# An encoder trunk with 64 experts: gate and up weights as one load of 16 KB a partition instead of two of 8 KB, expert rows read back four at a time

## The chip, the cores and the metric

One core of a Trainium2 chip runs the whole program. The metric is the device time of one execution in microseconds; the time of a kernel is the median of several runs.

## The reference, cut to what matters

Two layers over 512 tokens of width 1024, all in float32. Each layer has a token mixer (attention and spatial gating, not touched here) and a mixture of experts:

```python
scores = sigmoid(xt @ router_w)              # 512 tokens, 64 experts
sel = scores + router_bias                   # best 4 of 8 groups, then best 8 experts
wts = scores[eidx] / sum * 2.5
hb = silu(xb @ w_gate[e]) * (xb @ w_up[e])   # 1024 -> 256, for the tokens of expert e
yb = (hb @ w_down[e]) * wts                  # 256 -> 1024
routed = segment_sum(yb, token)
shared = (silu(xt @ ws_gate) * (xt @ ws_up)) @ ws_down
x = layer_norm(ALPHA * x + gate2 * (routed + shared), ln2_g, ln2_b)
```

Every expert has 2 MB of gate and up weights and 1 MB of down weights, so a layer's experts are 192 MB.

## The kernel before, in words

The instruction order of every engine is the order in which the program is written (`manual_schedule`); the tile framework adds the semaphores. All weight loads are issued by SyncE, one after the other, each waiting until the buffer that it overwrites has been read for the last time.

**Units.** The experts, ranked by load, have fixed capacities (`CAPS`). `_units` packs them into 43 units of 128 token rows: a unit is one expert with 128 rows, or two experts that share the rows (64 and 64, or 96 and 32). An expert with more than 128 rows, or one whose rows are cut, lies in two neighbouring units. The order of the units is set by `_units` from the planner's figures of line 49, so that units with much to load alternate with units with little: one unit of one expert stands at the front (`FIRSTS`), three at the end (`ENDS`).

**A unit's work** is in the loop of lines 1188 to 1221, one unit ahead in its first half: step `u_` does gate/up of unit `u_` and down of unit `u_ - 1`. In order on TensorE: at even steps the transposes of a pair's gathered rows (`turn_pair`, line 1025) and the slot matmuls of a later pair (`bring_pair`, line 1041, which also starts that pair's gathers on GpSimd, line 1046); gate/up over the first four of eight slices of 128 input columns (`gate_up` with half 0, line 770); the transposes of the unit before (`turn`, line 783); gate/up over the other four slices; then the down matmuls of the unit before (`down`, line 796). ScalarE and VectorE make silu and product (lines 775, 777), VectorE scales the result (line 802), and GpSimd scatters the rows to DRAM, one row for each token and choice (`ysl`, line 1062).

**Loads.** `get(r, part)` (line 760) loads a part of an expert's weights the first time that it is asked for: parts 0 and 1 are the two halves of gate and up, each 128 partitions of 8 KB, and part 2 is down, 128 partitions of 8 KB. `gate_up` asks for part 0 ahead of its first half and for part 1 ahead of its second (line 766), `down` for part 2 (line 791). SyncE so issues, for a step, the first halves of the unit's experts, their second halves, and the down weights of the unit before. The first eight loads of a layer are issued earlier, as soon as the experts' order is known (`AHEAD`, line 938).

**Buffers** (`wnew`, line 740). Gate/up tiles take turns in six buffers of 8 KB a partition (`w` in pool `bring`) and, once the overflow loop of line 1122 is past, two more (`w2` in pool `ch`, `MORE`). Down tiles have three buffers of 8 KB (`wd`). The router's weights take one of the six (line 690), the shared expert's gate and up two.

**Read-back.** After the last scatter that counts, `collect` (line 1178) loads the eight rows of each token again, two rows of 1024 at a time: 16 loads of 128 partitions of 8 KB, in the gate/up buffers. For each of the four token tiles (line 1236) VectorE adds the rows of the first two loads (line 1246), TensorE sums the other two by identity matmuls (line 1250) with the last two units' rows (line 1242), and VectorE adds that and normalises. In layer 1 the rows of the norm's weights are loaded after the read-back (lines 1227 and 1228), and VectorE and GpSimd apply them (lines 1232 and 1233).

Of the kernel before, what the change touches and what calls it, by code (L numbers as in the profile page):

```python
# [12 lines left out]
F32 = mybir.dt.float32  # L13
# [14 lines left out]
TOP = 8  # L28
# [11 lines left out]
PRE = 1  # L40
FIRSTS = 1
ENDS = 3
MORE = 2
AHEAD = 8
assert len(CAPS) == E


# [79 lines left out]
UNITS = _units()  # L127
# [48 lines left out]
def trunk(tc, A):  # L176
    nc = tc.nc
# [13 lines left out]
    act, dve, gp, pe = nc.scalar, nc.vector, nc.gpsimd, nc.tensor  # L191
# [9 lines left out]
    ident = kc[:, C_ID:C_ID + 128]  # L201
# [142 lines left out]
    def mixer(l, st):  # L344
# [54 lines left out]
        if l == 0:  # L399
            load, add, total = st["ada"]  # L400
            ws = [t[:, k] for t in (am.tile([128, 4, 2, 512], F32, tag="oa", name="wa1"),
                                    att.tile([128, 4, 2, 512], F32, tag="T16a", name="wa0")) for k in range(4)]
# [10 lines left out]
        if l == 0:  # L413
            ps = psum()
# [97 lines left out]
        for kv in range(2):  # L512
            for part in range(2):
                ps = psum(F32R)
# [172 lines left out]
        att.release()  # L687
        bring = pool("bring", "right")
        st["bring"] = bring
        t = bring.tile([128, 2048], F32, tag="w", bufs=6, name="rw")  # L690
        rw, rb = t[:, 0:NK * E].rearrange("p (k e) -> p k e", k=NK), t[:, NK * E:(NK + 1) * E]
        gp.dma_start(rw, A["router_w"][l])
        gp.dma_start(rb, A["router_bias"][l:l + 1, :].to_broadcast([128, E]))
# [28 lines left out]
    def moe(l, st):  # L722
# [17 lines left out]
        def wnew(part):  # L740
            if part == 2:
                return bp.tile([128, 2048], F32, tag="wd", bufs=WD_BUFS, name="wd")
            if more:
                more[0] += 1
                if more[0] % (6 + MORE) >= 6:
                    return more[1].tile([128, 2048], F32, tag="w2", bufs=MORE, name="we")
            return bring.tile([128, 2048], F32, tag="w", bufs=6, name="we")

        def load(which, part):
            t = wnew(part)  # L750
            if which == "shared":
                src = A["w_sh"][l, part]
            else:
                if which not in regs:
                    regs[which] = nc.sync.value_load(eid[0:1, which:which + 1], min_val=0, max_val=E - 1)  # L755
                src = A["w_exp"][l, ds(regs[which], 1), part].rearrange("o p n -> p (o n)")
            nc.sync.dma_start(t, src)  # L757
            return t

        def get(r, part):  # L760
            if (r, part) not in weights:
                weights[r, part] = load(r, part)
            return weights[r, part]

        def gate_up(xT, segs, half, ps):
            ws = [get(r, half) for r, _, _, _ in segs]
            for kk in range(4):
                k = half * 4 + kk
                for s, c, m in _tiles(segs):
                    pe.matmul(ps[c:c + m, :], xT[:, k, c:c + m], ws[s][:, kk * 512:(kk + 1) * 512],  # L770
                              start=k == 0, stop=k == NK - 1)

        def swiglu(ps, n):
# [49 lines left out]
        def shared_down(i):  # L823
            down(sh_h[i], SH, 128, None, ysh[:, i])

        for part in range(3):
            get("shared", part)
        pss = turn_x(range(NK))
        for i in range(NT):
# [105 lines left out]
        pe.matmul(pr[0:1, 0:E], kc[0:E, C_ECOL:C_ECOL + 1], perm[0:E, 0:E], start=True, stop=True)  # L935
        pe.matmul(pr[0:E, 64:65], perm[0:E, 0:E], ck[0:E, 1:2], start=True, stop=True)
        dve.tensor_copy(eid, pr[0:1, 0:E])
        for r, part in [(s[0], part) for u in UNITS[:3] for s in u for part in range(3)][:AHEAD]:
            get(r, part)
        px = psum()  # L940
        for i in range(NT):
# [180 lines left out]
        with tc.For_i(0, nov, 1) as j:  # L1122
            rv = dve.value_load(ovr[0:1, ds(j, 1)], min_val=0, max_val=E - 1)
            rs_ = nc.sync.value_load(ovr[0:1, ds(j, 1)], min_val=0, max_val=E - 1)
            dve.tensor_copy(cur, PW[:, :, ds(rv, 1)].rearrange("p i o -> p (i o)"))
            dve.tensor_copy(off, ovo[:, ds(j, 1)])
            dve.tensor_scalar(cur, cur, off, None, op0=OP.subtract)
            es = nc.sync.value_load(eid[0:1, ds(rs_, 1)], min_val=0, max_val=E - 1)
            for part in range(3):
                t = wnew(2) if part == 2 else ch.tile([128, 2048], F32, tag="w2", bufs=MORE, name="we")  # L1130
                nc.sync.dma_start(t, A["w_exp"][l, ds(es, 1), part].rearrange("o p n -> p (o n)"))
                weights["over", part] = t
            segs = [("over", 0, 0, 128)]
            P = bp.tile([128, NT, 256], F32R, tag="P", bufs=2, name="P")
            onehot(segs, P, 0, lambda r: cur[:, :, None])
            wc, idx, _ = slots(P, 0, segs, rv, rowbuf[:, 0])
            xg = bp.tile([128, NK, 256], F32, tag="xg", bufs=2, name="xg")
            gather([rowbuf[:, 0]], xg)
            ps = psum()
            gate_up(xg[:, :, 0:128], segs, 0, ps)  # L1140
            gate_up(xg[:, :, 0:128], segs, 1, ps)
            t = turn(swiglu(ps, 128), 128)
            y = down(t, segs, 128, wc)
            scatter(y, idx)
# [33 lines left out]
        def collect():  # L1178

            for i in range(NT):  # L1180
                for a in range(TOP // 2):
                    t = wnew(0).rearrange("p (j d) -> p j d", j=2)
                    src = ysl[l].rearrange("(t j) d -> t j d", j=TOP)
                    nc.sync.dma_start(t, src[i * 128:(i + 1) * 128, 2 * a:2 * a + 2, :])
                    got.append(t)

        got = []
        for u_ in range(n_units + 1):
            if u_ % 2:
                mark_pair(u_ // 2 + 3)  # L1190
            else:
                if u_:
                    turn_pair(u_ // 2 + 1) if units_of(u_ // 2 + 1) else None
                bring_pair(u_ // 2 + 2)
            if u_ < n_units:
                ps = psum()
                xT = G[u_][0]
                gate_up(xT, UNITS[u_], 0, ps)
            if u_ >= 1:
                t = turn(H[u_ - 1], rows_of(UNITS[u_ - 1]))  # L1200
            if u_ < n_units:
                gate_up(xT, UNITS[u_], 1, ps)
                H[u_] = swiglu(ps, rows_of(UNITS[u_]))
            if u_ == 0:
                turn_pair(1)
            if u_ >= 1:
                _, wc, idx, tk = G.pop(u_ - 1)
                if u_ - 1 >= n_units - LATE:
                    PT = late_mark(tk)
                y = down(t, UNITS[u_ - 1], rows_of(UNITS[u_ - 1]), wc)  # L1210
                if u_ - 1 < n_units - LATE:
                    scatter(y, idx)
                else:
                    late(y, PT)
                if u_ == n_units - LATE:
                    for v_ in range(u_, n_units):
                        for r, _, _, _ in UNITS[v_]:
                            for part in range(3):
                                get(r, part)
                    collect()  # L1220
                drain(slow, 3)
# [12 lines left out]
            nc.sync.dma_start(A["out"][i * 128:(i + 1) * 128, :], x[:, i])  # L1234

        for i in range(NT):
            mine = got[i * TOP // 2:(i + 1) * TOP // 2]
            fin = [psum() for _ in range(2)]
            for n, (PT, yg) in enumerate(lates):
                for a in range(2):  # L1240
                    for h in range(2):
                        pe.matmul(fin[h], PT[:, i * 128:(i + 1) * 128], yg[:, a, h * 512:(h + 1) * 512],  # L1242
                                  start=n == 0 and a == 0, stop=False)
            for t in mine[:2]:
                for j in range(2):
                    dve.tensor_tensor(x[:, i], x[:, i], t[:, j], op=OP.add)  # L1246
            for n, t in enumerate(mine[2:]):
                for j in range(2):
                    for h in range(2):
                        pe.matmul(fin[h], ident, t[:, j, h * 512:(h + 1) * 512], start=False, stop=n == 1 and j == 1)  # L1250
            for h in range(2):
                hs = slice(h * 512, (h + 1) * 512)
                dve.tensor_tensor(x[:, i, hs], fin[h], x[:, i, hs], op=OP.add)
            normalise(x[:, i], [x[:, i, h * 512:(h + 1) * 512] for h in range(2)], 1e-5, True, both=i == NT - 1)
            if last and i:
                affine(i - 1)
# [80 lines left out]
def _pack(inputs):  # L1337
# [21 lines left out]
    def expert(g, u, d):  # L1359
        lead = g.shape[:-2]  # L1360
        n = len(lead)
        gu = np.concatenate([g.reshape(*lead, 2, 4, 128, 256), u.reshape(*lead, 2, 4, 128, 256)], -1)
        gu = np.moveaxis(gu, n + 2, n + 1).reshape(*lead, 2, 128, 2048)
        dd = np.moveaxis(d.reshape(*lead, 1, 2, 128, 1024), n + 2, n + 1).reshape(*lead, 1, 128, 2048)
        return np.concatenate([gu, dd], n)

    out = {
        "kc": _consts(),
# [13 lines left out]
        "lnc": np.stack([f(n).reshape(L, NK, 128) for n in ("ln1_g", "ln1_b", "ln2_g", "ln2_b")], 1)  # L1382
        .transpose(3, 0, 1, 2).reshape(128, L * 4 * NK),
        "router_bias": f("router_bias"),
        "w_exp": expert(f("w_gate"), f("w_up"), f("w_down")),
        "w_sh": expert(f("ws_gate"), f("ws_up"), f("ws_down")),
    }
    return {k: np.ascontiguousarray(v) for k, v in out.items()}

# [11 lines left out]
```

## Time and profile before

| | before |
|---|---|
| median of 3 runs | 2148.94 us (2147.86 to 2150.25) |
| profiled execution | 2151.45 us, its span 2149.7 us |
| TensorE busy (PE) | 1999.3 us, 93% |
| weight loads of TensorE busy (PEld) | 1109.6 us, 52% |
| VectorE busy (DVE) | 1001.3 us, 47% |
| ScalarE, GpSimd busy (ACT, POOL) | 495.6 and 372.8 us |
| mean granted TensorE clock | 0.978 of full speed |
| loads of expert weights | 384 of 1 MB (256 of gate/up, 128 of down) |
| read-back loads | 32 of 1 MB |
| bytes moved by DMA | 626.30 MB |

The expert stages lie at about 455 to 1040 us (layer 0) and 1497 to 2077 us (layer 1); ahead of each is a mixer and the routing. Busy times are of engines, not of the chain that sets the end. A row such as `PE ps L770 <- DMA we<-in_w_exp` reads: TensorE's instruction of line 770, which writes `ps`, waited until the load of `we` from `in_w_exp` had landed. `q1` is SyncE's DMA queue, `q0` GpSimd's (gathers and scatters), and each load is spread over 16 DMA engines.

### The profile page before, as it was taken

Reading aid. Unit: us, or ns where it says so; the run is one execution under the profiler, and the core shown is the slowest. Engines: PE = TensorE matmul, PEld = TensorE weight load, DVE = VectorE, ACT = ScalarE, POOL = GpSimd, SP = SyncE. Lnnn points to the kernel's source line nnn. Section 1 sums busy time; section 2 is a strip of 40 time slices with the busy share of each in tenths; the row PEclk is TensorE's granted clock in tenths of the full one; section 3 lists DMA queues with packets and bytes.
Section 4 is the critical chain, followed back from the end, with each engine's and each line's share of the span. In section 5 each row is a group of like instructions: output and inputs, shape, how many; then the busy total and the mean of one; then the engine's idle time right before and its main releaser. Section 6 shows DMA issues by size and latency. Waiting matters only on the chain. (4 is left out here: it accounts for less than half of the span.)

```text
span 2149.7 us, 29249 instructions
## 1 busy us (share of the span) xinstructions
PE 1999.3 (93%) x10868; PEld 1109.6 (52%) x10868; DVE 1001.3 (47%) x2155; ACT 495.6 (23%) x983; POOL 372.8 (17%) x353
## 2 busy tenths in 40 slices
PE   5999999989999999999999999998999999999993
PEld 4888888443333433233488888854433334333341
DVE  6777857443332332222678665653333223232245
ACT  3464232111111111111145633321111111111110
POOL 1101101027111111111230010111631111111113
PEclk9999999989999999999999999998999999999997
DMA  7513665458999999999953045525899999999983
GB/s 276 186 40 119 211 210 197 160 209 359 408 404 407 422 392 406 417 410 376 391 177 118 16 154 164 192 78 210 349 405 408 409 410 421 392 411 401 419 363 155
DMA packets 120128, 626.30 MB, mean 291 GB/s; under 512 B 19472, under 2 KB 19472, under 8 KB 65968
## 3 DMA queue, kind: packets, MB, share of 16 engines
q1 hardware_dynamic: 92912, 550.99, 65.2%
q0 software_dynamic: 27072, 73.42, 9.2%
q8 instruction: 87, 1.43, 0.3%
q14 instruction: 57, 0.47, 0.1%
HBM read 596.02 MB, written 51.38 MB: 301 GB/s over the span
## 5 line engine op out<-in xcount | busy, mean ns | idle before, releaser
L770 PE MATMUL ps<-we,xg 128*32 128x512 f32 (+2 forms) x3648 | 670.0, 602 | 28.9 <-DMA we<-in_w_exp 28.7
L770 PEld LDWEIGHTS ps<-we,xg 128*32 128x32 f32 (+2 forms) x3648 | 210.1, 124 | 385.0 <-issue 295.4
L796 PE MATMUL ps<-wd,hTt 128*32 128x512 f32 (+2 forms) x1888 | 374.5, 603 | 25.9 <-DMA wd<-in_w_exp 22.6
L777 DVE TENSOR_TENSOR h<-h,ps 128x256 f32<-128x256 f32 x94 | 39.6, 421 | 597.7 <-ACT h L775 597.7
L796 PEld LDWEIGHTS ps<-wd,hTt 128*32 128x32 f32 (+2 forms) x1888 | 118.7, 127 | 259.0 <-issue 200.0
L1062 POOL DMA_INDIRECT ysl<-y,ii x82 | 88.1, 1075 | 788.0 <-DVE y L802 717.4
L802 DVE SCALAR_TENSOR_TENSOR y<-ps,wc,r 128x512 f32<-128x512 f32 x172 | 129.2, 751 | 201.3 <-PE ps L796 201.3
L299 PE MATMUL ps<-wH,hH 128*128 128x512 f32 (+1 forms) x512 | 197.1, 385 | 4.1 <-ACT hH L194 4.1
L300 PE MATMUL ps<-wL,hH 128*128 128x512 f32 (+1 forms) x512 | 194.8, 380 | 0.0
L301 PE MATMUL ps<-wH,hL 128*128 128x512 f32 (+1 forms) x512 | 194.5, 380 | 0.0
L194 ACT ACTIVATE hTt<-ps 128x256 f32<-128x256 f32 x94 | 36.1, 384 | 497.5 <-PE ps L783 497.5
L194 ACT ACTIVATE wH<-w 128x1024 fp32r<-128x1024 f32 x83 | 87.8, 1060 | 204.0 <-PE ps L301 129.7
L1032 ACT ACTIVATE xg<-ps,f 128x256 f32<-128x256 f32 (+1 forms) x176 | 84.2, 557 | 213.3 <-DVE xg L1034 213.3
L1046 POOL DMA_INDIRECT rowbuf<-xd,it x86 | 87.9, 1022 | 227.7 <-DVE it L1045 187.9
L296 DVE TENSOR_TENSOR wL<-w,wH 128x1024 fp32r<-128x1024 f32 x84 | 102.5, 1221 | 51.7 <-ACT wH L194 51.7
L775 ACT ACTIVATE h<-ps 128x256 f32<-128x256 f32 x94 | 36.1, 384 | 346.4 <-PE ps L770 346.4
L237 DVE SCALAR_TENSOR_TENSOR acc<-wa,cond,acc 128x1024 f32<-128x1024 f32 x80 | 106.7, 1333 | 9.5 <-DMA wa<-in_w_ada 4.8
L299 PEld LDWEIGHTS ps<-wH,hH 128*128 128x128 f32 x512 | 97.8, 191 | 23.9 <-ACT hH L194 5.2
L301 PEld LDWEIGHTS ps<-wH,hL 128*128 128x128 f32 x512 | 97.6, 191 | 18.8 <-DVE hL L296 0.9
L300 PEld LDWEIGHTS ps<-wL,hH 128*128 128x128 f32 x512 | 98.0, 191 | 17.9 <-issue 0.5
L1025 PEld LDWEIGHTS ps<-kc,rowbuf 128*128 128x128 f32 x688 | 75.9, 141 | 34.5 <-PE ps L796 17.4
L1025 PE MATMUL ps<-kc,rowbuf 128*128 128x128 f32 x688 | 84.1, 275 | 3.6 <-DMA rowbuf<-xd,it 3.6
(326 smaller groups left out, 2378.4 us busy)
## 6 DMA issues: line engine op xcount, KB each, us to landing
we<-in_w_exp SPq DMA_DIRECT2D x256, 1024.0 KB, 17.6
wd<-in_w_exp SPq DMA_DIRECT2D x128, 1024.0 KB, 16.6
wa<-in_w_ada SPq DMA_DIRECT2D x96, 512.0 KB, 4.5
w<-in_wA SPq DMA_DIRECT2D x92, 512.0 KB, 4.3
we<-ysl SPq DMA_DIRECT2D x32, 1024.0 KB, 12.4
we<-in_w_sh SPq DMA_DIRECT2D x4, 1024.0 KB, 9.4
xd<-x SPq DMA_DIRECT2D x8, 512.0 KB, 2.6
x<-in_x SPq DMA_DIRECT2D x4, 512.0 KB, 10.8
```

What stands on the lines that cost most here:

```text
L194: return act.activation(out, in_, AF.Copy)
L237: dve.scalar_tensor_tensor(acc, w, cond[:, k:k + 1], acc, op0=OP.mult, op1=OP.add)
L296: dve.tensor_sub(l_out, src, h_out.bitcast(F32))
L299: pe.matmul(ps, aH, wH, start=first, stop=False)
L300: pe.matmul(ps, aH, wL, start=False, stop=False)
L301: pe.matmul(ps, aL, wH, start=False, stop=last)
L770: pe.matmul(ps[c:c + m, :], xT[:, k, c:c + m], ws[s][:, kk * 512:(kk + 1) * 512], start=k == 0, stop=k == NK - 1)
L796: pe.matmul(ps[c:c + m, :], t[:, j, c:c + m], ws[s][:, j * 1024 + nh * 512:j * 1024 + (nh + 1) * 512], start=j == 0, stop=j == 1)
L802: dve.scalar_tensor_tensor(y[0:n, hs], ps[0:n], wcol[0:n], gate2[0:n, hs], op0=OP.mult, op1=OP.mult)
L1025: pe.transpose(ps[:, kk * 256 + b_ * 128:kk * 256 + (b_ + 1) * 128], r[:, (k2 * 2 + kk) * 128:(k2 * 2 + kk + 1) * 128], ident)
L1046: gp.indirect_dma_start(out=row, out_offset=None, in_=xd, in_offset=IndirectOffsetOnAxis(ap=it[:, 0:1], axis=0), bounds_check=T - 1, oob_i ...
L1062: gp.indirect_dma_start(out=ysl[l], out_offset=IndirectOffsetOnAxis(ap=ii[:, 0:1], axis=0), in_=y, in_offset=None, bounds_check=T * TOP - ...
```

## The change

Gate and up of an expert are packed as one array, so that a partition holds the eight slices of 512 columns in 16 KB, and down is an array of its own. A gate/up tile is 16 KB a partition; there are three and one of them instead of six and two. `gate_up` asks for the whole tile ahead of its first half. The first loads of a layer are five (three of 2 MB, two of 1 MB) instead of eight. The read-back loads four rows at a time, so a token tile has two loads: one for VectorE, one for TensorE.

```diff
-MORE = 2
-AHEAD = 8
+MORE = 1
+AHEAD = 5
...
-        t = bring.tile([128, 2048], F32, tag="w", bufs=6, name="rw")
+        t = bring.tile([128, 4096], F32, tag="w", bufs=3, name="rw")
...
                 more[0] += 1
-                if more[0] % (6 + MORE) >= 6:
-                    return more[1].tile([128, 2048], F32, tag="w2", bufs=MORE, name="we")
-            return bring.tile([128, 2048], F32, tag="w", bufs=6, name="we")
+                if more[0] % (3 + MORE) >= 3:
+                    return more[1].tile([128, 4096], F32, tag="w2", bufs=MORE, name="we")
+            return bring.tile([128, 4096], F32, tag="w", bufs=3, name="we")
...
             t = wnew(part)
+            of = "gu" if part == 0 else "d"
             if which == "shared":
-                src = A["w_sh"][l, part]
+                src = A["w_sh_" + of][l]
...
-                src = A["w_exp"][l, ds(regs[which], 1), part].rearrange("o p n -> p (o n)")
+                src = A["w_exp_" + of][l, ds(regs[which], 1)].rearrange("o p n -> p (o n)")
...
-            ws = [get(r, half) for r, _, _, _ in segs]
+            ws = [get(r, 0) for r, _, _, _ in segs]
...
-                    pe.matmul(ps[c:c + m, :], xT[:, k, c:c + m], ws[s][:, kk * 512:(kk + 1) * 512],
+                    pe.matmul(ps[c:c + m, :], xT[:, k, c:c + m], ws[s][:, k * 512:(k + 1) * 512],
...
-        for part in range(3):
+        for part in (0, 2):
             get("shared", part)
...
-                for a in range(TOP // 2):
-                    t = wnew(0).rearrange("p (j d) -> p j d", j=2)
+                for a in range(TOP // 4):
+                    t = wnew(0).rearrange("p (j d) -> p j d", j=4)
                     src = ysl[l].rearrange("(t j) d -> t j d", j=TOP)
-                    nc.sync.dma_start(t, src[i * 128:(i + 1) * 128, 2 * a:2 * a + 2, :])
+                    nc.sync.dma_start(t, src[i * 128:(i + 1) * 128, 4 * a:4 * a + 4, :])
...
-            mine = got[i * TOP // 2:(i + 1) * TOP // 2]
+            mine = got[2 * i:2 * i + 2]
...
-            for t in mine[:2]:
-                for j in range(2):
+            for t in mine[:1]:
+                for j in range(4):
                     dve.tensor_tensor(x[:, i], x[:, i], t[:, j], op=OP.add)
-            for n, t in enumerate(mine[2:]):
-                for j in range(2):
+            for t in mine[1:]:
+                for j in range(4):
                     for h in range(2):
-                        pe.matmul(fin[h], ident, t[:, j, h * 512:(h + 1) * 512], start=False, stop=n == 1 and j == 1)
+                        pe.matmul(fin[h], ident, t[:, j, h * 512:(h + 1) * 512], start=False, stop=j == 3)
```

The same two parts instead of three are asked for in the first loads (line 938), in the overflow loop (line 1129) and ahead of the read-back (line 1218). On the host `expert` (line 1359) returns the two arrays.

## Rows read from the trace of the kernel before

**Rows 1.** The page, part 2: busy tenths in 40 slices.

```profile
PE   5999999989999999999999999998999999999993
...
DMA  7513665458999999999953045525899999999983
```

**Rows 2.** Transfers, 530 to 1020 us: GB/s in 40 slices; queue: packets, MB, share.

```profile
GB/s 405 422 417 424 364 420 424 421 380 385 423 419 423 355 426 422 420 422 418 421 421 351 353 423 421 369 419 413 410 422 422 396 421 409 410 421 423 372 406 287
...
q1 hardware_dynamic: 23469, 170.90, 84.7%
q0 software_dynamic: 10151, 26.80, 13.8%
```

**Rows 3.** Waits of PE, 530 to 1020 us: total us, times, longest.

```profile
PE ps L770 <- DMA we<-in_w_exp: 14.2, 12, 2.4
PE ps L796 <- DMA wd<-in_w_exp: 11.2, 9, 2.2
```

**Rows 4.** Waits of SyncE's queue, 530 to 1020 us: total us, times, longest.

```profile
SPq L757 <- PE ps L796: 205.9, 29, 13.2
```

**Rows 5.** SyncE's issues, 560 to 600 us: start, us from first to last.

```profile
568.45 0.86 SPq L757 DMA_DIRECT2D we<-in_w_exp  x2
569.55 15.25 SPq L757 DMA_DIRECT2D wd<-in_w_exp  x2
```

**Rows 6.** Timeline of PE, 560 to 600 us: start, us, what, [idle before].

```profile
570.71 5.34 PE L770 MATMUL ps<-we,xg 128*64 128x512 f32 x14 [2.42 <-DMA we<-in_w_exp]
575.98 0.44 PE L783 MATMUL ps<-kc,h 128*128 128x128 f32 x2
576.35 3.97 PE L770 MATMUL ps<-we,xg 128*64 128x512 f32 x16
...
581.63 3.65 PE L796 MATMUL ps<-wd,hTt 128*64 128x512 f32 x14 [0.78 <-DMA wd<-in_w_exp]
```

**Rows 7.** Transfers, 1040 to 1060 us (read-back alone): queue: packets, MB, share.

```profile
q1 hardware_dynamic: 1162, 8.47, 101.1%
```

**Rows 8.** Line 757 (weight loads), 520 to 1020 us: issue to landing.

```profile
DMA to landing us min/median/max: 5.2/18.7/26.3
```

**Rows 9.** Transfers, first 20 us: queue: packets, MB, share.

```profile
q1 hardware_dynamic: 2862, 6.08, 85.7%
```

**Rows 10.** SyncE's issues at other times.

```profile
340.63 0.86 SPq L757 DMA_DIRECT2D we<-in_w_sh  x2
...
461.15 3.77 SPq L757 DMA_DIRECT2D we<-in_w_exp  x2
...
499.46 19.18 SPq L757 DMA_DIRECT2D wd<-in_w_exp  x2
```

**Rows 11.** Timeline of PE at other times.

```profile
389.62 2.84 PE L770 MATMUL ps<-we,hT 128*128 128x512 f32 x6
...
453.79 2.03 PE L1041 MATMUL ps<-WT,P 128*128 128x196 f32 x8 [3.86 <-DVE P L1015]
...
479.93 3.62 PE L770 MATMUL ps<-we,xg 128*128 128x512 f32 x8
...
1069.52 7.13 PE L1250 MATMUL ps<-we,kc 128*128 128x512 f32 x16 [0.86 <-DMA we<-ysl]
...
2023.10 3.19 PE L796 MATMUL ps<-wd,hTt 128*32 128x512 f32 x25 [2.36 <-DMA wd<-in_w_exp]
```

**Rows 12.** Two stretches: busy us by engine (instructions), then clock, DMA share, GB/s.

```profile
450.00:462.00 12.00, 8.21 (x19) 4.69 (x20) 3.48 (x18) 2.00 (x5) 1.98 (x2) 0.72 0.24 71
...
571.00:581.00 10.00, 9.86 (x34) 3.53 (x30) 0.17 (x1) 0.77 (x2) 0.00 (x0) 0.83 1.02 424
```

**Rows 13.** The same view, 40 us of layer 1's expert stage.

```profile
1920.00:1960.00 40.00, 36.97 (x290) 15.14 (x286) 13.28 (x48) 6.30 (x16) 5.87 (x6) 0.96 0.98 408
```

**Rows 14.** Timeline of DVE near the end.

```profile
2111.82 0.83 DVE L1232 TENSOR_TENSOR x<-x,lnr 128x640 f32<-128x640 f32 x1 [14.10 <-DMA lnr<-in_ln_g]
```

**Rows 15.** Gathered rows, 530 to 1020 us: issue to landing.

```profile
DMA to landing us min/median/max: 8.9/10.8/14.0
```

More of the change, by code (lines that the diff above doesn't have):

```diff
@@ L937, in moe @@
         dve.tensor_copy(eid, pr[0:1, 0:E])
-        for r, part in [(s[0], part) for u in UNITS[:3] for s in u for part in range(3)][:AHEAD]:
+        for r, part in [(s[0], part) for u in UNITS[:3] for s in u for part in (0, 2)][:AHEAD]:
             get(r, part)
@@ L1128, in moe @@
             es = nc.sync.value_load(eid[0:1, ds(rs_, 1)], min_val=0, max_val=E - 1)
-            for part in range(3):
-                t = wnew(2) if part == 2 else ch.tile([128, 2048], F32, tag="w2", bufs=MORE, name="we")
-                nc.sync.dma_start(t, A["w_exp"][l, ds(es, 1), part].rearrange("o p n -> p (o n)"))
+            for part, of in ((0, "gu"), (2, "d")):
+                t = wnew(2) if part == 2 else ch.tile([128, 4096], F32, tag="w2", bufs=MORE, name="we")
+                nc.sync.dma_start(t, A["w_exp_" + of][l, ds(es, 1)].rearrange("o p n -> p (o n)"))
                 weights["over", part] = t
@@ L1217, in moe @@
                         for r, _, _, _ in UNITS[v_]:
-                            for part in range(3):
+                            for part in (0, 2):
                                 get(r, part)
@@ L1362, in expert @@
         gu = np.concatenate([g.reshape(*lead, 2, 4, 128, 256), u.reshape(*lead, 2, 4, 128, 256)], -1)
-        gu = np.moveaxis(gu, n + 2, n + 1).reshape(*lead, 2, 128, 2048)
-        dd = np.moveaxis(d.reshape(*lead, 1, 2, 128, 1024), n + 2, n + 1).reshape(*lead, 1, 128, 2048)
-        return np.concatenate([gu, dd], n)
+        gu = np.moveaxis(gu.reshape(*lead, 8, 128, 512), n + 1, n).reshape(*lead, 128, 4096)
+        dd = np.moveaxis(d.reshape(*lead, 2, 128, 1024), n + 1, n).reshape(*lead, 128, 2048)
+        return gu, dd
+    w_exp = expert(f("w_gate"), f("w_up"), f("w_down"))
+    w_sh = expert(f("ws_gate"), f("ws_up"), f("ws_down"))
     out = {
@@ L1384, in _pack @@
         "router_bias": f("router_bias"),
-        "w_exp": expert(f("w_gate"), f("w_up"), f("w_down")),
-        "w_sh": expert(f("ws_gate"), f("ws_up"), f("ws_down")),
+        "w_exp_gu": w_exp[0], "w_exp_d": w_exp[1],
+        "w_sh_gu": w_sh[0], "w_sh_d": w_sh[1],
     }
```

## The prediction

> **What bounds the kernel now.** I read the page's slices first. In both expert stages TensorE and the transfers are at nine tenths at once [rows 1], so neither share tells which one sets the pace. The transfer view of 530 to 1020 us does: the hardware queue takes 84.7% and the gather and scatter queue 13.8% of the 16 DMA engines [rows 2], together 98.5%, at some 420 GB/s wherever the queue is full. Then the waits of that stretch: what TensorE waits for is weights, 14.2 us in 12 waits ahead of gate/up and 11.2 us in 9 ahead of down [rows 3]. So weights arrive just in time, and the transfers are the bound. But the transfers hang on TensorE in turn: SyncE, which issues all loads in program order, was held 205.9 us in 29 waits by the down matmuls of line 796 [rows 4], because a third down tile has to be given back before the next down load, and the gate/up loads behind it, can go out. A later down matmul is a later load wherever the queue is nearly empty. The slices of [rows 2] show such places: without the last, which is cut by the stage's end, eight slices under 390 GB/s (364, 380, 385, 355, 351, 353, 369, 372), of which two pairs are neighbours, so six places a layer.
>
> **One place, step by step.** The down load of 569.55 us and the next one are one group of 15.25 us, so the second was issued at 569.55 + 15.25 - 0.33 = 584.5, after the down matmuls that began at 581.63 [rows 5, 6]. Still on their way were two gate/up loads (568.45) and one down load (569.55): 3 MB. A full queue moves 8.47 MB in 20 us [rows 7], 2.5 us for 1.05 MB, so from 581.6, when the awaited down tile landed, they last 7.5 us, to 589.1. An empty queue needs 5.2 us from issue to landing [rows 8], 2.7 of them before the data flow. 584.5 + 2.7 = 587.2, so 1.9 us of margin.
>
> **Costs, per layer.**
>
> *Packets saved.* 16 KB rows instead of 8 KB. With a per packet and B per MB, [rows 2] give 10151a + 26.80B = 13.8% of 16 x 490 = 1082 us and 23469a + 170.90B = 6640 us, so B = 38.0 us and a = 6.3 ns. A 1 MB load is 8 row packets and a completion packet on each engine (163 loads: 20864 + 2608 packets, the count of the row). Gate and up fall from 18 to 9 packets: 9 x 6.3 = 57 ns an expert, 3.6 us for 64, and 0.5 us for the eight pairs of read-back loads: **-4.1 us**. Bounds: nearly 0, if a 16 KB row still moves as two packets; above, the same two equations with the read-back and the first 20 us of the program, whose rows are 4 KB and less (1162a + 8.47B = 323.5 us, 2862a + 6.08B = 274.2 us [rows 7, 9]), give 20.7 ns and -13.4 us. I take 6.3 ns, which is from the stretch itself. Fewer issues save nothing: SyncE waits far more than it issues. The Trainium skill ("DMA: Bandwidth & Descriptors", section "Anatomy of one DMA — SWDGE (gpsimd) path") fits each DMA of the GpSimd path with a fixed 2.0 us; charged to these loads, 72 fewer would give 144 us a layer, an estimate from that page. The trace disagrees for a full queue: 2.5 us for a whole load leaves no room for 2.0 us that nothing hides.
>
> *The wider wait.* Before, TensorE starts a unit on its first halves and needs the second halves 4.0 us later (3.65 for the half and some 0.4 for the turn of line 783 [rows 6]). Now it starts when all of it is there. In a unit of two experts the second halves land 5 us after the first, so where weights come just in time the end of gate/up moves from 3.6 to 7.6 us after the last landing: 4.0 later. The down matmuls that follow would have waited 11.2 / 9 = 1.25 us anyway, so they are 2.75 us later. At the place above: half 1 began at 576.35 and took 3.97 instead of 3.65, so all was there by about 576.5; now gate/up ends at 584.1 instead of 580.3, and down begins there instead of at 581.63: 2.5 later. Of 2.75 the margin covers 1.9; 0.85 us of empty queue remains, six times: **+5.1 us**. Bounds: 0, if the margin holds everywhere; 16.5 if there is none. The buffers themselves are the same 11 MB. That a first half's buffer comes back a half later costs nothing in the steady stage, since SyncE is by then held by a down tile whose matmuls come after both halves. At the layer's start the load of 461.15 had its partner issued 3.4 us later and must now wait that long itself; the pair is needed at 479.93, and between 499.46 and 518.3 SyncE issues nothing, so the queue runs empty there anyway and the start is forgotten [rows 10, 11].
>
> *The clock.* The two waits of such a unit become one long one: at the place above at least from 568.3 (570.71 less 2.42) to 576.5 us. After 2.42 us of waiting the granted clock already fell there, to 0.83 over 10 us: 1.7 us lost. Around a wait of 3.86 us before 453.79 it was 0.72 over 12 us [rows 6, 11, 12]. Such falls in the expert stages are four in both layers, the first that of [rows 12], the last that of [rows 13]; the waits for weights of 2.1 to 2.6 us were nine, the first at 570.71, the last before 2023.10 [rows 6, 11]. So a short wait is followed by a fall about every other time, a longer one more often. I take four of the six places; the margin is used up there, so each is 1.7 us more: **+6.8 us**. Bounds: 0 and 10.2. The Trainium skill ("TensorE: Matmul & The Clock Gate", section "HAM oscillation — how this bites in real kernels") has matmul bursts between DMA waits start cold each time, which speaks against this change; by it all six fall.
>
> *Read-back and end.* Eight 2 MB tiles instead of 16. The last identity matmuls began at 1069.52, right after a wait for a tile, and ran 7.13 us [rows 11]; the last 1 MB landed 2.5 us after that tile. Both are now one: 1069.5 + 2.5 - 0.5 = 1071.5, so **+2.0 us** in layer 0. In layer 1 VectorE waited 14.10 us for the norm's rows [rows 14], queued behind the read-back, so the end moves with the queue: **-0.5 us**. VectorE's four adds of a token tile come from one load instead of two; in layer 1 they stand behind that wait, in layer 0 behind the tile before, so they cost nothing.
>
> *Edits at nothing.* The shared expert's wider load goes out at 340.6 and is first used at 389.62 [rows 10, 11]. The router's tile takes one of three buffers instead of one of six, so the prefetch stays at 8 MB in the same order of bytes. The weights' new layout is made on the host. Gathers must now share engines with packets twice as long: 10.8 us to land at the median, 14.0 at most [rows 15]; at twice the median they would still land within the two units, some 25 us, by which they are brought ahead of their transposes. Scatters land likewise ahead of any reuse.
>
> **Sum.** Per layer 5.1 + 6.8 - 4.1 = 7.8, twice 15.6, with +1.5 for the ends 17.1 us. The profiled execution took 2151.45 us around its span of 2149.7, 2.5 us above the median of 2148.94; the sum is made in its durations and put on the median: **2166 us**.
>
> **Rivals.**
> 1. *Faster.* At most places the margin is in truth more than 2.75 us, not 1.9, because TensorE makes up the half it starts later while the queue is full, and no clock falls. It decides at the down matmuls of a unit whose successor but one brings a single new expert (3 MB in the queue). Then -4.1 twice, +1.5: 2142 us; with 20.7 ns a packet 2124. For: 98.5% of the DMA time is used, so shorter packets are shorter time. Against: the six slices.
> 2. *Cancelled.* Places cost half (2.5), no clock: 2149 - 2 x 1.6 + 1.5 = 2147 us.
> 3. *Smaller loss.* Places as forecast, clock kept: 2 x (5.1 - 4.1) + 1.5 = 3.5, 2152 us.
> 4. *Doesn't do what it says.* The 16 KB row is still moved as two packets: 2166 + 8 = 2174 us.
> 5. *Larger loss.* No margin and six falls: 16.5 + 10.2 - 4.1 = 22.6, twice and +1.5: 2196 us.
>
> **Chances.** Forecast 0.45 (its own range 2156 to 2178), faster 0.17, cancelled 0.09, smaller loss 0.16, two packets 0.06, larger loss 0.07. About 0.2%, 4.3 us, can be told from no change: faster 0.17, the same 0.17 (cancelled, and half of the smaller loss, whose place is at that edge), slower 0.66. The range leaves out the deeper half of the faster case and most of the larger loss: 2143 to 2188.
>
> **What would show it.** Right: 8 KB packets of the hardware queue replaced by 16 KB ones in gate/up, fewer bytes per second in the six slices though the full queue is faster than 424; PE's waits for gate/up longer and fewer, those for down weights nearly gone; more slices with a clock under 1.00 in the expert stages; SyncE still held by line 796. Wrong: the same idle time of PE with a shorter stage (rival 1), packet counts unchanged (rival 4), or a gather that PE's line 1025 waits for, which I cost at nothing.

## The result and the profile after

| | before | after |
|---|---|---|
| median of 4 runs | 2149.09 us | 2165.45 us (2164.5 to 2166.98) |
| ratio to before, 95% interval | | 1.0074 [1.0061, 1.0088] |
| profiled execution, its span | 2151.45, 2149.7 us | 2166.98, 2165.1 us |
| mean granted TensorE clock | 0.978 | 0.969 |

Slower by 0.74%, 16 us, and within 1 us of the forecast's total. The page's slices of the changed kernel (they answer to [rows 1]):

```profile
PE   5999999989999999889999999998999999998994
...
DMA  7513665469999999989953045525999999999983
```

Two rows of its timelines place the loss: the last identity matmuls of layer 0, and VectorE's wait for the norm's rows near the end.

```profile
1079.38 7.13 PE L1251 MATMUL ps<-we,kc 128*128 128x512 f32 x16 [0.85 <-DMA we<-ysl]
```

```profile
2127.30 0.83 DVE L1233 TENSOR_TENSOR x<-x,lnr 128x640 f32<-128x640 f32 x1 [12.05 <-DMA lnr<-in_ln_g]
```

Against 1069.52 [rows 11] and 2111.82 [rows 14], layer 0 lost 9.9 us up to there and layer 1, with its mixer, 5.6 more. The forecast had 9.8 and 7.3.

Transfers, 530 to 1020 us (GB/s in 40 slices; queue: packets, MB, share), beside [rows 2]:

```profile
GB/s 412 423 422 415 385 431 425 422 383 424 431 397 311 402 421 428 426 420 423 430 413 347 420 425 380 385 426 330 393 428 420 309 422 267 326 419 415 373 407 264
...
q1 hardware_dynamic: 15284, 166.76, 82.1%
q0 software_dynamic: 9990, 26.36, 13.6%
```

A row is one packet of 16 KB now, so the packets fell. A full queue is faster (up to 431 GB/s where it had been 420 to 426), and the gaps are deeper: 267, 309, 311 GB/s where the lowest had been 351 (the last slice, cut by the stage's end, left out in both). Together the queues use 95.7% of the DMA time instead of 98.5%.

Waits in the same stretch, TensorE's, then those of SyncE's queue (total us, times, longest), beside [rows 3, 4]:

```profile
PE ps L771 <- DMA we<-in_w_exp_gu: 35.0, 14, 5.3
```

```profile
SPq L758 <- PE ps L797: 306.4, 32, 19.1
SPq L758 <- PE ps L771: 70.2, 11, 10.4
```

TensorE no longer waits for down weights; it waits longer for gate/up. SyncE is held longer by the down matmuls, 306.4 us instead of 205.9. One place shows the turn of it. Timelines of TensorE and SyncE in the kernel before, then in the changed one:

```profile
928.93 3.62 PE L770 MATMUL ps<-we,xg 128*32 128x512 f32 x32
...
937.79 4.18 PE L796 MATMUL ps<-wd,hTt 128*32 128x512 f32 x31
```

```profile
929.16 12.35 SPq L757 DMA_DIRECT2D wd<-in_w_exp  x2
```

```profile
926.86 1.03 PE L771 MATMUL ps<-we,xg 128*32 128x512 f32 x6
933.24 6.41 PE L771 MATMUL ps<-we,xg 128*32 128x512 f32 x26 [5.35 <-DMA we<-in_w_exp_gu]
...
943.41 3.62 PE L797 MATMUL ps<-wd,hTt 128*32 128x512 f32 x32
```

```profile
927.08 20.29 SPq L758 DMA_DIRECT2D wd<-in_w_exp_d  x2
```

Line 770 could run on the unit's first halves at once. The changed kernel, after six matmuls on the expert that is there, must have the other one whole: 5.35 us of waiting, its down matmuls 5.6 us later than before, and the second down load, which waits for them, goes out at 947 instead of 941. The next row (busy times, then granted clock, DMA share, GB/s) has the rest of that place:

```profile
928.00:938.00 10.00, 4.76 (x24) 1.17 (x25) 1.08 (x2) 0.00 (x0) 1.21 (x1) 0.70 1.01 418
938.00:948.00 10.00, 10.00 (x82) 3.40 (x78) 2.05 (x4) 0.77 (x2) 0.00 (x0) 0.96 0.41 172
```

The granted clock is 0.70 over the ten microseconds of the wait and its end: part of them ran at 1.2 instead of 2.4 GHz. While TensorE works that off, the queue runs empty: 172 GB/s, where the kernel before moved 390 in the same ten microseconds. Such a fall of the granted clock is called a clock fall below. From the first gate/up to the last down matmuls the two expert stages have 13 of them, 8 and 5, where the kernel before had 4; a fourteenth lies in the read-back of layer 1.

### The profile page after: what moved, and what is told of

Its sections match the earlier page's. It is cut to its first block, busy times and chain, and to the rows that moved or that the text cites. A ratio compares the mean times of both kernels' runs of the same rounds, so it can differ in the third digit from the quotient of the medians.

```text
span 2165.1 us, 28772 instructions
## 1 busy us (share of the span) xinstructions
PE 2002.0 (92%) x10868; PEld 1105.8 (51%) x10868; DVE 1013.3 (47%) x2155; ACT 495.1 (23%) x983; POOL 371.1 (17%) x353
## 5 line engine op out<-in xcount | busy, mean ns | idle before, releaser
L771 PE MATMUL ps<-we,xg 128*32 128x512 f32 (+2 forms) x3648 | 682.3, 620 | 69.6 <-DMA we<-in_w_exp_gu 69.6
L797 PE MATMUL ps<-wd,hTt 128*32 128x512 f32 (+2 forms) x1888 | 346.8, 597 | 3.1 <-ACT hTt L194 3.1
L194 ACT ACTIVATE wH<-w 128x1024 fp32r<-128x1024 f32 x83 | 87.8, 1060 | 204.8 <-PE ps L301 132.8
```

The lines of the kernel that those rows point to most:

```text
L194: return act.activation(out, in_, AF.Copy)
L771: pe.matmul(ps[c:c + m, :], xT[:, k, c:c + m], ws[s][:, k * 512:(k + 1) * 512], start=k == 0, stop=k == NK - 1)
L797: pe.matmul(ps[c:c + m, :], t[:, j, c:c + m], ws[s][:, j * 1024 + nh * 512:j * 1024 + (nh + 1) * 512], start=j == 0, stop=j == 1)
```

## The experiments

Ratios are to the kernel before, run beside them on the same chip; differences between experiments are differences of ratios times 2149 us. By the intervals of the ratios (95%, in brackets) such a difference is known to about 4 us, an estimate.

**e1_halves: the wait undone, the buffers kept.**

```diff
-AHEAD = 5
+AHEAD = 8
...
+            if part == 1:
+                t = weights[which, 0][:, 2048:4096]
...
+            if segs[0][0] != "over":
+                [get(r, half) for r, _, _, _ in segs]
             ws = [get(r, 0) for r, _, _, _ in segs]
```

> The changed kernel, but each 16 KB tile is filled by two loads of 8 KB rows, in the order of the kernel before (first halves of a unit's experts, then second halves, then down), and TensorE waits for each half by itself. Buffers stay 16 KB and come back whole, the read-back stays at four rows. Wider wait (the forecast): the loss of the expert stages goes and so does the packet saving, so only the ends are left, +1.5: 2147 to 2154 us, with 2 to 4 clock falls in the expert stages instead of 14, TensorE waiting again for down weights. Rival, coarse buffers: SyncE waited 70.2 us for line 771 in 530 to 1020 us where it had waited 23.2 us for line 770, because a buffer comes back a half later; then the starved queue stays and the packet saving of some 8 us goes: 2168 to 2175 us. In between, both count.

2145.43 us, 0.9983 [0.9974, 0.9992]. Below the expected span, and faster than the kernel before. Its waits in 530 to 1020 us, TensorE's and two of SyncE's:

```profile
PE ps L778 <- DMA we<-in_w_exp_gu: 13.2, 13, 2.1
PE ps L804 <- DMA wd<-in_w_exp_d: 12.1, 10, 2.3
```

```profile
SPq L763 <- PE ps L804: 196.0, 27, 13.2
...
SPq L763 <- PE ps L778: 59.4, 11, 6.4
```

TensorE's waits are those of [rows 3] again, with 4 clock falls, and SyncE is held by the down matmuls of line 804 no longer than in [rows 4]. It is still held 59.4 us by gate/up buffers that come back whole, and the kernel is none the slower for it: the rival of coarse buffers is out. The run takes back three things at once, the wait for whole tiles, the loads of 2 MB and the 16 KB packets; together they are the whole loss. The next runs part them.

**e2_packets and e5_near: 16 KB loads in 8 KB packets.** Two layouts of the host array; in the first the halves of a row lie 1 MB apart, in the second 512 bytes. The lines below end in the name of the run that has them.

```diff
...
-        gu = np.moveaxis(gu.reshape(*lead, 8, 128, 512), n + 1, n).reshape(*lead, 128, 4096)
+        gu = np.moveaxis(gu.reshape(*lead, 8, 128, 512), n + 1, n).reshape(*lead, 128, 2, 2048)
+        gu = np.moveaxis(gu, n + 1, n)                                       # e2_packets
+        gu = np.concatenate([gu, np.zeros_like(gu[..., 0:128])], -1)         # e5_near
```

> The changed kernel, with the same loads of 2 MB, waits and order, but the array on the host is laid out in two halves, so that a row of a partition comes as two packets of 8 KB. Packets by the forecast (6.3 ns each, 9 fewer an expert and engine): 3.6 us a layer without the eight read-back loads, 2 x 3.6 = 7.2 us above the changed kernel's 2165.5, so 2169 to 2176 us, if the queue sets the pace. Rival, packets cost nothing on the path (the queue has idle time in its starved places and takes the longer packets there): 2164 to 2168 us. The clock falls should not move by more than two.

> Follows from e2_packets, which was 36 us slower than the changed kernel where 7.2 was forecast; its two halves of a row lay 1 MB apart in DRAM. Here the same two packets of 8 KB a row and partition lie side by side, 512 bytes apart, all else as in the changed kernel. Packets set it (the first halves lie no better than the second, only the count and size of the packets matter): about as e2_packets, 2190 to 2206 us. Rival, the place in DRAM set it: by the forecast's 7.2 us for packets 2169 to 2176 us.

2201.74 us, 1.0249 [1.0231, 1.0266], and 2204.65 us, 1.0258 [1.0244, 1.0272]. e2_packets missed both its expectations, and e5_near met the larger of its two: against the changed kernel, packets of half the size cost 38 and 40 us, not 7.2, wherever the halves lie. The clock falls rose from 13 to 18 and 19. Waits and transfers of e5_near in 530 to 1020 us:

```profile
PE ps L774 <- DMA we<-in_w_exp_gu: 46.8, 15, 6.2
```

```profile
GB/s 417 421 418 411 259 423 425 417 293 371 421 423 408 255 399 424 422 419 421 419 422 413 238 392 423 335 371 423 369 330 422 414 353 408 408 203 406 426 341 385
```

The full queue is back at some 422 GB/s, which is the small part. The gaps are deeper and come earlier: in the first half of the stretch, where the changed kernel's lowest slice was 311, three are now below 300.

**e7_wait_alone: the wider wait without the change's loads.**

```diff
+            if segs[0][0] != "over":
+                [get(r, 0) for r, _, _, _ in segs]
+                [get(r, 1) for r, _, _, _ in segs]
...
+            if half == 0 and segs[0][0] not in ("over", "shared"):
+                for w in ws:
+                    pe.matmul(ps[0:32, 0:4], ident[:, 0:32], w[:, 2048:2052], start=True, stop=True)
```

> The kernel of e1_halves (loads of 1 MB, packets of 8 KB), but the second halves are asked for right behind the first, and a matmul of 4 columns on each second half, into the tile that gate/up then starts anew, makes TensorE wait for all halves ahead of gate/up. So the wider wait comes alone, without the loads of 2 MB and their packets. Forecast's sizes (wait and clock without the packet saving): 2145.4 + 20 for what e1_halves gave back + 7.2 = 2170 to 2177 us. Rival, with the wider wait every longer packet time shows at each place (as e2_packets had it): 2190 to 2206 us. If the wait is not the cause: 2145 to 2152 us.

2209.06 us, 1.0281 [1.0267, 1.0295]. That is 3 us above the second expectation and 32 above the first. Against e1_halves the difference is 0.0298 x 2149 = 64 us, and it is not the wait alone: the matmuls that make TensorE wait take time themselves. Where nothing is waited for, they put most of gate/up off by 0.15 us:

```profile
598.07 0.26 PE L778 MATMUL ps<-we,kc 128*32 128x4 f32 x3
...
598.22 2.31 PE L782 MATMUL ps<-we,xg 128*32 128x512 f32 x17
```

If each of the 86 units of both layers pays that and no more, it is 13 us, an estimate, and some 51 us are left for the wait. e5_near, which has no such matmuls but loads of 2 MB, is 59 us above e1_halves. Both show that waiting for whole tiles, with 8 KB packets, costs far more than the forecast had; whether loads of 1 or of 2 MB make a difference of some us is not told.

**e4_warm and e11_warm_8k: the clock kept up.** Matmuls whose result is thrown away, inside the waits of the changed kernel and of e5_near.

```diff
+                for _ in range(WARM.get(u_, 0)):
+                    pe.matmul(ps, ident, kc[:, 0:512], start=True, stop=True)
...
+WARM = {19: 3, 27: 3, 32: 2, 33: 3, 35: 3, 37: 3}                                            # e4
+WARM = {9: 3, 13: 3, 17: 2, 19: 3, 27: 3, 30: 3, 32: 3, 33: 2, 35: 3, 37: 3}                 # e11
```

> The changed kernel with 2 or 3 further matmuls (128x512, 0.9 us each) into a PSUM tile that the next matmul starts anew, ahead of gate/up of units 19, 27, 32, 33, 35 and 37, where TensorE waits 2 to 5 us for weights in both layers. They run inside the wait. Clock as forecast (each fall 1.7 us on the path): if the falls at these places go, some 9 of 14, about 15 us come back at most, 2150 to 2160 us. Rival, the falls are covered (what TensorE loses after a wait it makes up while the queue is full, and the queue sets the end): 2163 to 2168 us with fewer falls. If the falls stay as many, this run says nothing of their price.

> The kernel of e5_near with 2 or 3 further matmuls (as in e4_warm) ahead of gate/up of units 9, 13, 17, 19, 27, 30, 32, 33, 35 and 37, where it waits 2 to 6 us. It has 19 clock falls in the two expert stages. By e4_warm, where 11 falls fewer gave 6.1 us, 0.55 us each: 2191 to 2198 us. By the forecast's price, 1.7 us each: 2170 to 2178 us. If the falls are all of what 8 KB packets cost: about the changed kernel, 2165 us.

2159.39 us, 1.0049 [1.0035, 1.0062], and 2184.54 us, 1.0169 [1.0152, 1.0185]. The same stretch of the two layers (third number from the end: granted clock), in e4_warm, e5_near and e11_warm_8k:

```profile
530.00:1020.00 490.00, 470.02 (x2917) 180.16 (x2915) 137.37 (x413) 66.90 (x171) 72.44 (x70) 0.99 0.97 401
1580.00:2060.00 480.00, 461.95 (x2904) 178.16 (x2903) 136.28 (x411) 66.12 (x169) 73.05 (x70) 1.00 0.98 405
```

```profile
530.00:1020.00 490.00, 443.24 (x2778) 166.93 (x2780) 131.30 (x402) 63.85 (x163) 71.67 (x69) 0.95 0.95 384
1580.00:2060.00 480.00, 435.24 (x2652) 165.78 (x2652) 134.73 (x417) 63.31 (x162) 80.69 (x73) 0.95 0.95 386
```

```profile
530.00:1020.00 490.00, 465.37 (x2872) 177.92 (x2871) 134.54 (x408) 65.29 (x167) 73.39 (x70) 0.98 0.96 389
1580.00:2060.00 480.00, 460.35 (x2823) 177.05 (x2822) 135.47 (x419) 66.38 (x169) 78.95 (x73) 0.99 0.97 395
```

The falls go from 13 to 2 (two more lie in the read-backs) and from 19 to 7. In the changed kernel that gives back 0.0025 x 2149 = 5.4 us, 0.5 us a fall; in e5_near 19 us, 1.6 us a fall. By the intervals of the ratios these are 0.1 to 0.9 and 1.2 to 2.0 us a fall, an estimate, and they are what is left after whatever the further matmuls cost. So a fall did not have one price. That it costs what it makes late, and so more in e5_near, whose queue moved less (384 against 395 GB/s in the changed kernel), is argued, not shown. e4_warm lies inside the first of its expectations, at its upper end; e11_warm_8k missed all three of its own.

**e3_mixed and e8_places: the wide wait in part of the units.**

```diff
+        HALVES = {s[0] for u in UNITS[27:] for s in u} - {s[0] for u in UNITS[:27] for s in u}  # e3_mixed
...
+                if n in (9, 13, 17, 19, 27, 30, 32, 33, 35, 37, 40):                             # e8_places
+                    HALVES.add(r)
...
+            cols = slice(2048, 4096) if part == 1 else slice(0, 2048 if part == 2 or which in HALVES else 4096)
```

> The changed kernel for units 0 to 26; from unit 27 on a tile is filled by two loads of 8 KB rows as in the kernel before. Unit by unit the changed kernel's down matmuls gained 5.9 us (layer 0) and 4.7 us (layer 1) on the kernel before between units 0 and 25, and lost 14.3 and 6.3 us between units 25 and 40. Wider wait: the gain stays and the loss goes, 2149 - 10.6 + 1.5 for the ends = 2140, say 2136 to 2146 us, under the kernel before. Rival, coarse buffers: the loss of the second part stays at more than half, 2150 us or more. Rival, the gain of the first part is chance (two of its steps are clock falls of the kernel before that were missing): 2147 to 2152 us.

> The kernel of e3_mixed, but two loads of 8 KB rows only for the experts that come first in units 9, 13, 17, 19, 27, 30, 32, 33, 35, 37 and 40, ahead of which TensorE waited in the changed kernel in both layers; the other 43 experts come as one load. Wider wait at these places alone costs: the packet saving of 43 of 64 experts is kept without loss, 2145.4 - 2 x 2.4 = 2138 to 2142 us. Rival, taken from these places the wait moves to others, or the saving is nothing: 2144 to 2152 us.

2145.18 us, 0.9977 [0.9969, 0.9986], and 2148.89 us, 0.9999 [0.999, 1.0008]. e3_mixed lies in its expected span, below both rivals, but no lower than e1_halves, so in units 0 to 26 whole loads, their packets and their wider wait together, bring nothing over halves. e8_places missed the forecast's span and lies in its rival's. TensorE's waits there in 530 to 1020 us:

```profile
PE ps L785 <- DMA we<-in_w_exp_gu: 20.8, 12, 3.6
```

With the known places taken out, waits of 2.6 to 3.6 us stand ahead of units 21, 28 and 38 of layer 0, and the expert stages have 8 falls. The wait has moved to other whole loads.

**e6_readback: the read-back.** Two loads of two rows into each tile of e1_halves.

```diff
-                    nc.sync.dma_start(t, src[i * 128:(i + 1) * 128, 4 * a:4 * a + 4, :])
+                    for b in (0, 2):
+                        nc.sync.dma_start(t[:, b:b + 2], src[i * 128:(i + 1) * 128, 4 * a + b:4 * a + b + 2, :])
```

> The kernel of e1_halves, but the read-back loads two rows of 8 KB at a time again, two loads into each 16 KB tile, each awaited by itself. Forecast's term for the read-back (+2.0 and -0.5): 1.5 us less than e1_halves' 2145.4, 2142 to 2146 us. Rival, the wider read-back is what made e1_halves faster than the kernel before: 2147 to 2151 us.

2143.51 us, 0.9971 [0.9959, 0.9982], the fastest kernel of the study, 6 us under the one before. Against e1_halves it is 2.6 us less, the direction and about the size of the forecast's 1.5, but the two intervals overlap, so it is not told from nothing.

**e9_rows2k, e10_rows2k_16k, e12_rows2k_halves: gathers and scatters of half rows.**

```diff
+            for a in range(2):
...
+                dve.tensor_scalar(i2, ii, 2.0, float(a), op0=OP.mult, op1=OP.add)
+                gp.indirect_dma_start(out=ysl[l].rearrange("t (a d) -> (t a) d", a=2),
...
+                                      in_=y[:, a * 512:(a + 1) * 512],
```

> The kernel of e5_near, but each gather and each scatter is two, of half a row (packets of 2 KB instead of 4 KB on GpSimd's queue). In e4_warm, whose weights come in 16 KB packets, a gather took 15.2 us to land at the median, against 10.8 us in the kernel before with 8 KB packets: the two queues seem to take turns by the packet, so that large weight packets leave the gathers a smaller share. Turns by the packet: with 8 KB against 2 KB the shares are those of 16 KB against 4 KB, gathers land in 14 us or more, and most of the 39 us between e5_near and the changed kernel comes back; the 22,000 further packets at 9 ns, the length of one of 4 bytes, take some 12 us of 16 engines: 2165 to 2185 us. Rival, only the weights' own packets matter: 2204 us and up.

> The changed kernel with gathers and scatters of half rows as in e9_rows2k. Turns by the packet: the gathers' share falls again, 16 KB against 2 KB, weights at the waiting places land earlier still, 2150 to 2165 us. Rival, the further packets cost their time: 2166 to 2178 us.

> The kernel of e6_readback (two halves of 8 KB rows awaited each by itself, read-back by two rows, 2143.5 us) with gathers and scatters of half rows. Turns by the packet: the places where TensorE waits in that kernel (13.8 us in 14 waits for gate/up, 12.2 us in 8 for down in 530 to 1020 us) shorten, 2135 to 2143 us. Rival, there is no wait left that a gather lengthens, and the further packets cost their time: 2144 to 2156 us.

2344.9, 2408.32 and 2337.94 us (1.0903, 1.1202 and 1.0874): all far beyond either expectation. The waits of GpSimd and TensorE in e9_rows2k, 530 to 1020 us, say why:

```profile
POOL ysl L1072 <- DMA ysl<-y,i: 167.6, 31, 8.8
```

```profile
PE ps L1029 <- DMA rowbuf<-xd,it: 64.1, 32, 5.8
```

The second scatter of a unit waits until the first has landed, GpSimd stands still for it, the gathers behind it go out late, and TensorE waits for them; in the other two runs the same wait of GpSimd sums to 139.2 and 151.6 us. So these runs measure that wait, and nothing follows from them for the question of the packets' turns.

## Why the prediction was right, and where it was not

The total was right to 1 us, and that was luck. The mechanism was right in its direction: to wait for whole tiles costs time, and 16 KB packets give time back. But the first term was some 35 us too small and the second some 31 us, and the two errors cancel. For two layers:

| term | forecast | measured |
|---|---|---|
| wider wait with its clock falls | 2 x (5.1 + 6.8) = +23.8 | +59 (e5_near against e1_halves, with loads of 2 MB); +64 (e7_wait_alone against e1_halves, an estimated 13 of it from its further matmuls) |
| 16 KB packets | -8.2 | -40 (the changed kernel against e5_near) |
| read-back and ends | +1.5 | +2.6 (e1_halves against e6_readback, not told from 0) |
| buffers, start of the layers | 0 | -6 (e6_readback against before) |

These are the steps of one chain: before, e6_readback, e1_halves, e5_near, after. So the last three rows and +59 make 16 us by construction, and their sum confirms nothing. The step from e1_halves to e5_near changes the size of the loads and the number of first loads beside the wait; e7_wait_alone is the run that keeps these out.

*The wider wait.* The step from later down matmuls to later down loads to an empty queue is as forecast, and the rows of 926 to 948 us show it. Wrong were the places, and too small was what they cost. The forecast counted six places from slices below 390 GB/s of the kernel before and took a margin of 1.9 us from one of them, and its bound for wait and clock, 2 x (16.5 + 10.2) = 53.4 us, is under the 59 of e5_near. At the very place that it worked out it had one wait of 8 us and down matmuls 2.5 us later. The changed kernel there (TensorE's timeline, then the stretch after the wait):

```profile
568.10 3.65 PE L771 MATMUL ps<-we,xg 128*64 128x512 f32 x14 [2.03 <-DMA we<-in_w_exp_gu]
...
575.53 3.60 PE L797 MATMUL ps<-wd,hTt 128*64 128x512 f32 x16
```

```profile
571.00:581.00 10.00, 10.00 (x54) 4.34 (x53) 2.96 (x6) 1.32 (x4) 0.76 (x1) 1.00 0.95 384
```

The wait was 2.03 us, the clock stayed at 1.00 where it had been 0.83 [rows 12], and the down matmuls began 6.1 us earlier than the 581.63 of [rows 6]; 4 us of that had been gained at the start of the layer. In e5_near, which differs by its 8 KB packets alone, the same place has a wait of 4.24 us and a clock of 0.92 from 571 to 581 us. In the eight low slices of [rows 2] the rate did not fall either: it rose in seven, and fell from 351 to 347 in one. The new gaps lie beside them or where the kernel before had some 400 GB/s (423 to 311, 410 to 330, 396 to 309, 409 to 267). In layer 0 the loss comes late. The same transposes of `turn`, in the kernel before and in the changed one, at step 30 of layer 0 and at the last step:

```profile
849.79 0.44 PE L783 MATMUL ps<-kc,h 128*128 128x128 f32 x2
...
1033.72 0.38 PE L783 MATMUL ps<-kc,h 128*128 128x128 f32 x2
```

```profile
842.28 0.44 PE L784 MATMUL ps<-kc,h 128*128 128x128 f32 x2
...
1042.40 0.38 PE L784 MATMUL ps<-kc,h 128*128 128x128 f32 x2
```

The changed kernel was 7.5 us ahead at step 30 and 8.7 us behind at the end. So a slice of the kernel before shows where the queue was short with narrow waits, not where it will be. That a margin is used up from place to place, since a late down load makes the gate/up behind it late, would explain the late loss; it is argued, not shown. One more sign failed: TensorE's waits for gate/up became longer but not fewer, 14 instead of 12.

*The clock.* Four more falls a layer were forecast; five and four more came. The price of 1.7 us is what e5_near shows (1.6), in a queue that is often empty; in the changed kernel it was 0.5, so of the forecast's 13.6 us some 5 are there. The Trainium skill ("TensorE: Matmul & The Clock Gate", section "HAM oscillation — how this bites in real kernels") blames such waits for cold starts; the trace agrees that they bring falls (13 for 4), while the run that removed 11 of the 13 gave back a third of the loss.

*The packets.* Their own length was right. With a = 6.3 ns and B = 38.0 us the changed kernel's row should take 15284 x 0.0063 + 166.76 x 38.0 = 6433 us of 7840, 82.1%, and that is what it took. What failed is the step that set their worth equal to their length. With whole tiles awaited, 8 KB packets cost five times their length. Part of the 40 us comes by way of the clock: with most falls removed in both kernels (e11_warm_8k against e4_warm) the difference is 0.0120 x 2149 = 26 us. What 8 KB packets cost where halves are awaited apart, no run shows. And the larger packets do something that the forecast had as a risk only: they take more of the engines from the gathers. Transfers from 555 to 567 us, ahead of the wait for unit 9, in the changed kernel and in e5_near, two gathers having been issued at 555 to 558 in both, 1.4 us later in the changed kernel:

```profile
q1 hardware_dynamic: 333, 4.30, 83.9%
q0 software_dynamic: 207, 0.75, 15.7%
```

```profile
q1 hardware_dynamic: 492, 3.80, 75.7%
q0 software_dynamic: 416, 1.20, 25.0%
```

With 16 KB packets the weights moved 0.5 MB more in these 12 us, and gathers and scatters 0.45 MB less. Issue to landing of the gathers in e4_warm (16 KB packets) and in e11_warm_8k (8 KB), 530 to 1020 us:

```profile
DMA to landing us min/median/max: 8.5/15.2/18.5
```

```profile
DMA to landing us min/median/max: 8.8/10.3/11.2
```

Gathers land 5 us later, and as they are fetched far ahead TensorE waits for none of them in this stretch, which the forecast had right. The Trainium skill ("DMA: Bandwidth & Descriptors", section "Queues, rings and completion order") has each DMA engine take turns between queues by the packet, where a packet is several descriptors; these rows agree with it so far as the queue with the larger rows moves more, and do not show how much one turn holds. That this share, rather than the 57 ns saved for each expert, makes most of the 40 us is argued, not shown: the runs with half rows were to tell and could not.

*The start of the layers* was costed at nothing. TensorE's waits of the kernel before from 490 to 530 us:

```profile
PE ps L1025 <- DMA rowbuf<-xd,it: 2.4, 1, 2.4
```

This wait for a gather is gone in the changed kernel and in e6_readback; with the 1.2 us of the same wait in layer 1 it is 3.6 of the 6 us by which e6_readback is faster. Why the gather is in time there, and where the other 2 us come from, stays open.

*Rivals.* "Doesn't do what it says" is out by the packet count. "Faster" is what layer 0 looks like up to step 30, and the rest of the layer undid it. "Larger loss" (2196) is near what the wider wait makes with 8 KB packets, 2202 to 2209 us.

## What to carry to other kernels

In a kernel like this one, whose loads arrive just in time, ask for the unit of waiting before the unit of loading: one tile may be filled by two loads that are awaited apart, and that kept the larger buffer free of loss (0.9983, and 0.9971 with the smaller read-back). A right total says little of its terms, and two large errors can hide in it: change one thing at a time along the chain from the old kernel to the new one. Price a clock fall or a packet by a run that removes it, not by its own length.

## What was not expected of the hardware

- 8 KB instead of 16 KB packets cost 40 us of 2165, though the packets' own time differs by some 0.06 us an expert (9 x 6.3 ns, by [rows 2]); weights in 16 KB packets came with gathers of the other queue that took 15.2 instead of 10.3 us to land.
- A fall of the granted clock, removed by further matmuls, gave back 0.5 us in one kernel and 1.6 us in another with the same work.
- 17 discarded matmuls a layer, 0.9 us each, made the changed kernel 5 us faster; 28 made e5_near 19 us faster.
